# Second down projection token-major, two value groups projected together, attention queries by residue within each half

## The chip, the cores and the metric

The kernel runs on one core of a Trainium2 chip. The metric is device time in microseconds for one execution of the whole program, weights and activations coming from HBM. The engines are TensorE (PE, with its weight loads listed as PEld), VectorE (DVE), ScalarE (ACT), GpSimd (POOL) and SyncE (SP), whose queue issues most of the DMAs.

## The reference, cut to what matters

A two-layer decoder trunk on 256 tokens of 1024 channels, float32. Layer one is a Mamba-2 mixer and a gated FFN with a causal convolution; then keys and values are projected once; layer two is dilated attention and the same kind of FFN; a final RMSNorm gives the output.

```python
ATT_PATTERNS = ((128, 1), (512, 4), (2048, 16))     # window, dilation: three groups
# 8 heads and 2 key/value heads in each group, head size 128
...
for layer in range(DEPTH):
    ...
    x = x + _dilated_mixer(_rms_norm(x, b_norm[j]), k_sh, v_sh, att_w_q[j], att_w_o[j], positions)
    x = x + _conv_ffn(_rms_norm(x, ffn_norm[layer]), ffn_w_up[layer], ffn_conv_w[layer], ffn_w_down[layer])
return _rms_norm(x, final_norm)
```

In group 0 a query sees the last 129 tokens. In group 1 it sees earlier tokens with its own index modulo 4, in group 2 those with its own index modulo 16. One softmax runs over all three groups. The FFN has 2816 hidden channels (22 tiles of 128).

## The kernel before, in words

The residual stream `X` is held channel-major: 128 partitions x 8 channel tiles x 256 tokens. Every projection is exact to float32 by splitting both operands into a high and a low part (fp32r): each product is three matmuls, high x high, high x low, low x high. Weights come in 1 MB pieces (`raw`) by the SP queue and are split on chip by `split` (L93 to L98): ACT rounds the high part (L95), DVE subtracts for the low part (L97). Three `raw` buffers and six `wh`/`wl` pairs of 1024 columns rotate.

TensorE's order is written by hand in the program. The other engines' instructions are ordered by a list scheduler that takes what is ready, earliest in the program first.

**Down projection** (`res_proj`, L606): for both FFNs a stationary 128x128 weight tile meets all 256 tokens. The high weight takes the high and the low operand side by side, one matmul of 512 columns (L625), and the low weight takes the high operand, one of 256 columns (L627). `finish` (L642) adds the result to `X` and, in the second FFN, scales with the final norm's weight into `XW` (L652, L657) and squares. After the last tile `turn` transposes `XW` to token-major (16 transposes, L927), the sums of squares are reduced by small matmuls (L934), POOL takes the power (L942), ACT and DVE scale (L950, L947), and SP stores four blocks of 256 KB (L951).

**Values**: `v_mm(p)` projects one group's 256 value columns for both halves of the tokens, with 256-column matmuls (L262 to L264). Group 1 comes first, the last two channel tiles of both halves last (`late_last`), then the norm's statistics (`nm.stats`, L214), then groups 2 and 0. Groups 1 and 2 go to DRAM and are read back as `Vs`, by residue class modulo 4.

**Attention**: queries stand by residue modulo 4 over all 256 tokens (four classes of 64), so each half of 128 queries holds two classes. For each head `q_tile` projects three groups (24 matmuls of 256 columns each, L242 to L244), and `scores` (L849) computes, for each half, one matmul against all 256 keys of group 0 (L854) and four of 64 queries x 64 keys for groups 1 and 2 (L859), adds a mask and takes the maximum (L863), the exponential (L868) and the normalisation (L870). `p_transpose` (L873) makes three 128x128 transposes for each half (L878); `values` (L883) sums over group 0 with two matmuls of 256 columns (L888) and over groups 1 and 2 with four of 64 (L892), and ACT and DVE split the result into `OT` (L895, L896). Attention operands are plain float32; each of their matmuls is listed as two. TensorE's order around head h is:

```python
q_tile(h, hs[h], 0)
if h > 1:
    p_transpose(h - 2, hs[h - 2])
q_tile(h, hs[h], 1)
if h:
    scores(h - 1, hs[h - 1])
q_tile(h, hs[h], 2)
if h > 1:
    values(h - 2, hs[h - 2])
```

The last two heads' steps are hooks inside the output projection `w_o`, whose `finish` puts its result back into token order.

Of the kernel before, what the change touches and what calls it, by code (L numbers as in the profile page):

```python
# [12 lines left out]
T = 256  # L13
# [15 lines left out]
for _g in range(NG):  # L29
# [3 lines left out]
        ("final_norm", 8), ("ssm_norm", 16), ("dt_bias", 32), ("a_log", 32), ("dskip", 32),  # L33
# [3 lines left out]
_ATT = [("mask", 768), ("cos", 256), ("sin", 256), ("cosp", 256), ("sinp", 256)]  # L37
# [15 lines left out]
def trunk(ctx, tc, a, out):  # L53
# [46 lines left out]
    class Weights:  # L100


        def __init__(self):
# [5 lines left out]
            self.seq += [(("w_v", p), a["w_v"][p], 1024) for p in (1, 2, 0)]  # L109
# [8 lines left out]
        def ffn(self, L):  # L118
            self.seq += [((f"w_up{L}", j), a[f"w_up{L}"][j], 1024) for j in range(FT)]
            self.res(f"w_down{L}", FT)  # L120
# [54 lines left out]

    class Stream:


        def __init__(self, ws):
            self.ws = ws  # L180
            self.h = []
            self.l = []
            for i in range(len(ws)):
# [4 lines left out]
        def add(self, k):  # L188
            for i, w in enumerate(self.ws):
                h, l, x = self.h[i][:, k, :], self.l[i][:, k, :], X[:, k, :]  # L190
                if w == "b_norm":
                    h, l, x = by_class(h), by_class(l), x.rearrange("p (i r) -> p i r", r=4)
                hi_lo(h, l, x, P(w)[:, k:k + 1])
# [60 lines left out]
    def tile_b(po, units, xh, xl, n, c, ks=range(KT), clear=True, **kw):  # L254

        t = slice(c * 128, c * 128 + 128)
        kper = KT // len(units)
# [348 lines left out]
    def res_proj(w, nk, operand, late, S, facc=None, perm=False, first=2, hooks={}):  # L606
# [35 lines left out]
        def finish(n, ys):  # L642
            x = X[:, n, :]
            if perm:
                x = x.rearrange("p (i r) -> p i r", r=4)
            for y in ys:
                DVE.tensor_tensor(out=x, in0=by_class(y) if perm else y, in1=x, op=ALU.add)  # L647
            x = X[:, n, :]
            if S is not None:
                S.add(n)  # L650
            elif n < KT - 1:
                ACT.activation(out=XW[:, n, :], in_=x, func=AF.Copy, scale=P("final_norm")[:, n:n + 1])  # L652
                add_sq(facc, n)
            else:
                lastsq.append(wk.tile([128, T], F32, tag="sq", name="sq"))
                ACT.activation(out=lastsq[0], in_=x, func=AF.Square)
                DVE.tensor_scalar(out=XW[:, n, :], in0=x, scalar1=P("final_norm")[:, n:n + 1],  # L657
                                  scalar2=None, op0=ALU.mult)
# [27 lines left out]
    lastsq = []  # L686
    XW = None

    def ffn(L, S, nxt, facc=None):
        nonlocal XW  # L690
# [28 lines left out]
        for j in range(FT):  # L719
# [11 lines left out]
            if j == 1:  # L731
                ops.append(normed(f"ffn_norm{L}", nm.row))
        if nxt is None:
            XW = act.tile([128, KT, T], F32, tag="xh0", name="XW")
        res_proj(f"w_down{L}", FT, lambda k: g[k // 2][:, k % 2 * 2:k % 2 * 2 + 2, :],
                 [20, 21], nxt, facc)
# [6 lines left out]

    accp = act.tile([128, T], F32, tag="sqp", name="accp")
    DVE.tensor_copy(out=by_class(accp), in_=SA.acc.rearrange("p (i r) -> p i r", r=4))
# [3 lines left out]
    mask = act.tile([128, 2, 384], F32, tag="dec8", name="mask")  # L749
    SP.dma_start(out=mask.rearrange("p c s -> p (c s)"), in_=a["att"][:, :768])  # L750
    trig = act.tile([32, 1024], F32, tag="dec9", name="trig")
    SP.dma_start(out=trig, in_=a["att"][0:32, 768:])

    def C(n):
        return trig[:, ATT[n][0] - 768:ATT[n][1] - 768]

# [12 lines left out]
    def k_post(p, po):  # L769
        kt = KTt[p]  # L770
        sx = "p" if p else ""
        for i in range(2):
            d, x, y = kt[:, i, :], po[:, i, :], nm.row
            if p:
                d = by_class(d)
                x, y = (v.rearrange("p (i r) -> p i r", r=4) for v in (x, y))
            DVE.tensor_tensor(out=d, in0=x, in1=y, op=ALU.mult)
        sh = wk.tile([32, 2, T], F32, tag="cvxs", name="shk")
        DVE.stream_shuffle(out=sh, in_=kt[0:32], mask=rot)
        sn, cs = (C(n + sx).unsqueeze(1).to_broadcast([32, 2, T]) for n in ("sin", "cos"))  # L780
# [4 lines left out]
    def v_mm(p):  # L785
        us, po = W.get("w_v", p), acc_bank()
        if p == 1:
            late_last(lambda c, **kw: tile_b(po[:, c, :], us, xh, xl, 256, c, **kw))
            return po
# [4 lines left out]
    def v_post(p, po):  # L794
        vt = V0
        if p:
            vt = wk.tile([128, 2, T], F32, tag="cvbc", name="vt")
        for c in range(2):
            ACT.activation(out=vt[:, c, :], in_=po[:, c, :], func=AF.Copy, scale=nm.col[:, c:c + 1])
            if p:  # L800
                SP.dma_start(out=vd[128 * c:128 * c + 128, 256 * (p - 1):256 * p], in_=vt[:, c, :])
        if p:
            SP.dma_start(out=Vs[64 * (p - 1):64 * p],
                         in_=vd.rearrange("(i r) f -> i r f", r=4)[:, :, 256 * (p - 1):256 * p])

    po = v_mm(1)
    nm.stats()
    v_post(1, po)
    po = v_mm(2)
    nm.bcast()  # L810
    v_post(2, po)
    v_post(0, v_mm(0))
# [35 lines left out]

    def scores(h, st):  # L849
# [217 lines left out]
```

## Time and profile before

| what | value |
|---|---|
| time, median of 3 runs | 794.57 us (794.43 to 795.48) |
| the profiled execution's own time | 796.08 us |
| its span, first to last instruction | 794.3 us |
| busy: PE, PEld | 774.3 us (97%), 742.7 us (94%) |
| busy: DVE, ACT, POOL | 619.5 us (78%), 478.6 us (60%), 160.6 us (20%) |
| chain that ended last, by engine | PE 75%, DVE 11%, POOL 4%, ACT 4%, issue 3%, DMA 2% |

The chain that ended last is followed back from the last instruction. Busy time of PE is that of overlapping instructions; the distance between the starts of two neighbouring matmuls is what one costs in a dense stretch.

### The profile page before, as it was taken

The numbers are of one execution on the slowest core, as the hardware profiler recorded it, in microseconds if no ns is written. First come the engines' busy times: TensorE is split into PE (matmuls) and PEld (weight loads), VectorE is DVE, ScalarE is ACT, GpSimd is POOL, SyncE is SP. The second block draws the span as 40 slices with busy tenths as digits, with TensorE's granted clock in tenths as the row PEclk, the third lists the DMA queues.
The fourth block names the chain that finished last, engine by engine and source line by source line (L and its number), as shares of the span: only waits on it lengthen the run. The fifth ranks groups of instructions, "written<-read, shape, count | busy, mean of one in ns | idle before, by whom it ended". The sixth has DMA issues, their size and how long they took to land.

```text
span 794.3 us, 14954 instructions
## 1 busy us (share of the span) xinstructions
PE 774.3 (97%) x5992; PEld 742.7 (94%) x5992; DVE 619.5 (78%) x1004; ACT 478.6 (60%) x806; POOL 160.6 (20%) x141
## 2 busy tenths in 40 slices
PE   8999799999999999999999999999999999999997
PEld 7898799999989999999889999999999999999886
DVE  5888979788496999887677598878668999887551
ACT  7846568777375776655555446555466766565441
POOL 0323436543324400000011032211124300000010
PEclk9999989999999999999999999999999999999999
DMA  8484543363454366554556644334325465545521
GB/s 296 169 321 165 203 153 106 109 212 113 154 201 171 106 238 213 186 183 163 196 179 225 222 160 156 115 129 159 108 61 205 149 226 209 199 160 177 177 85 53
DMA packets 22886, 135.31 MB, mean 170 GB/s; under 512 B 2529, under 2 KB 4097, under 8 KB 8865
## 3 DMA queue, kind: packets, MB, share of 16 engines
q1 hardware_dynamic: 21616, 130.14, 47.0%
q10 hardware_dynamic: 1200, 4.23, 1.5%
q8 instruction: 47, 0.77, 0.4%
q14 instruction: 23, 0.18, 0.1%
HBM read 132.75 MB, written 1.61 MB: 169 GB/s over the span
## 4 chain that ended last, share of the span: by engine, by line
PE 75%; DVE 11%; POOL 4%; ACT 4%; issue 3%; DMA 2%; SPq 0%; DVEq 0%; ACTq 0%; POOLq 0%
PE po L242 15%; PE po L243 15%; PE po L244 15%; PE po L625 12%; PE po L627 6%; DVE wl L97 6%; PE po L633 4%; DVE cv L286 2%; PE s L854 1%; DVE xl L169 1%; POOL rs L537 1%; PE py L524 1%; PE op L888 1%; ACT wh L95 1%; PE op L892 1%
## 5 line engine op out<-in xcount | busy, mean ns | idle before, releaser
L97 DVE TENSOR_TENSOR wl<-raw,wh 128x1024 fp32r<-128x1024 f32 (+1 forms) x242 | 307.8, 1278 | 64.0 <-ACT wh L95 63.1
L95 ACT CAST wh<-raw 128x1024 fp32r<-128x1024 f32 (+1 forms) x242 | 247.7, 1034 | 170.5 <-PE po L243 87.0
L243 PE MATMUL po<-xnl,wh 128*128 128x256 f32 x800 | 227.0, 284 | 1.1 <-DVE xnl L319 1.1
L242 PE MATMUL po<-xnh,wh 128*128 128x256 f32 x800 | 227.0, 284 | 0.0
L244 PE MATMUL po<-xnh,wl 128*128 128x256 f32 x800 | 227.0, 284 | 0.0
L242 PEld LDWEIGHTS po<-xnh,wh 128*128 128x128 f32 x800 | 152.8, 191 | 0.3 <-issue 0.2
L243 PEld LDWEIGHTS po<-xnl,wh 128*128 128x128 f32 x800 | 151.2, 189 | 1.3 <-DVE xnl L319 1.3
L244 PEld LDWEIGHTS po<-xnh,wl 128*128 128x128 f32 x800 | 151.2, 189 | 0.1
L625 PE MATMUL po<-gp,wh 128*128 128x512 f32 x352 | 123.3, 393 | 0.0
L286 DVE SCALAR_TENSOR_TENSOR cv<-po,prm,cv 128x255 f32<-128x255 f32 (+2 forms) x232 | 105.8, 476 | 14.1 <-ACT cv L282 12.6
L242 PE MATMUL po<-xh,wh 128*128 128x256 f32 x400 | 115.0, 288 | 0.0
L243 PE MATMUL po<-xl,wh 128*128 128x256 f32 x400 | 113.2, 283 | 0.5 <-DVE xl L169 0.5
L244 PE MATMUL po<-xh,wl 128*128 128x256 f32 x400 | 113.0, 283 | 0.0
L627 PE MATMUL po<-gp,wl 128*128 128x256 f32 x352 | 98.5, 280 | 0.0
L625 PEld LDWEIGHTS po<-gp,wh 128*128 128x128 f32 x352 | 66.0, 187 | 15.4
L242 PEld LDWEIGHTS po<-xh,wh 128*128 128x128 f32 x400 | 76.3, 191 | 0.6
L243 PEld LDWEIGHTS po<-xl,wh 128*128 128x128 f32 x400 | 76.0, 190 | 0.7 <-DVE xl L169 0.7
L244 PEld LDWEIGHTS po<-xh,wl 128*128 128x128 f32 x400 | 75.9, 190 | 0.0
L627 PEld LDWEIGHTS po<-gp,wl 128*128 128x128 f32 x352 | 66.2, 188 | 0.0
L202 POOL TENSOR_TENSOR sqacc<-sqacc,sq 128x256 f32<-128x256 f32 x21 | 19.9, 946 | 217.0 <-ACT sq L201 216.7
L647 DVE TENSOR_TENSOR X<-po,X 128x256 f32<-128x256 f32 x52 | 20.9, 420 | 24.4 <-PE po L627 17.4
L202 POOL TENSOR_TENSOR facc<-facc,sq 128x256 f32<-128x256 f32 x6 | 4.5, 752 | 157.6 <-ACT sq L201 157.6
(207 smaller groups left out, 1270.4 us busy)
## 6 DMA issues: line engine op xcount, KB each, us to landing
raw<-w_up SPq DMA_DIRECT2D x44, 1024.0 KB, 4.8
raw<-w_down SPq DMA_DIRECT2D x16, 1024.0 KB, 4.8
raw<-w_xs SPq DMA_DIRECT2D x8, 1024.0 KB, 4.8
raw<-w_bc SPq DMA_DIRECT2D x8, 1024.0 KB, 4.8
raw<-w_out SPq DMA_DIRECT2D x8, 1024.0 KB, 4.8
raw<-w_q SPq DMA_DIRECT2D x8, 1024.0 KB, 5.1
raw<-w_z SPq DMA_DIRECT2D x7, 1024.0 KB, 6.2
raw<-w_down SPq DMA_DIRECT2D x8, 768.0 KB, 4.2
```

The costliest lines, as they stand in the source:

```text
L95: ACT.copy(out=wh[:, :n], in_=raw)
L97: DVE.tensor_tensor(out=wl[:, :n], in0=raw, in1=wh[:, :n].bitcast(F32), op=ALU.subtract)
L169: DVE.scalar_tensor_tensor(out=xl, in0=x, scalar=w, in1=xh.bitcast(F32), op0=ALU.mult, op1=ALU.subtract)
L202: POOL.tensor_tensor(out=acc, in0=acc, in1=sq, op=ALU.add)
L242: PE.matmul(po, lhsT=wh, rhs=xh, start=start, stop=False, **kw)
L243: PE.matmul(po, lhsT=wh, rhs=xl, start=False, stop=False, **kw)
L244: PE.matmul(po, lhsT=wl, rhs=xh, start=False, stop=stop, **kw)
L286: r = DVE.scalar_tensor_tensor(out=dst[:, i, s:], in0=u[:, i, :T - s], scalar=w[i][:, taps - 1 - s:taps - s], in1=dst[:, i, s:], op0=ALU.m ...
L625: PE.matmul(p.rearrange("p c t -> p (c t)"), lhsT=wh[:, c], rhs=y.rearrange("p c t -> p (c t)"), start=st, stop=False, skip_group_check=True)
L627: PE.matmul(p[:, 1, :], lhsT=wl[:, c], rhs=y[:, 0, :], start=False, stop=sp, skip_group_check=True)
L633: PE.matmul(p[:, o, :], lhsT=l[:, c], rhs=y[:, x, :], start=st and q == 0 and not o, stop=sp and q == 2, skip_group_check=True)
L647: DVE.tensor_tensor(out=x, in0=by_class(y) if perm else y, in1=x, op=ALU.add)
```

## The change

The second FFN's down projection turns its operands round: 128 tokens of the hidden activation are stationary and 512 output channels move, for each of two channel halves, 22 hidden tiles and two token halves, three matmuls of 512 columns each (264 in all). Its result is token-major, so `X` is transposed instead of `XW`: 16 transposes, four after each of the up projection's tiles 6 to 9. The last block of hidden tiles is finished for tokens 0 to 127 first and then for 128 to 255. The final norm's weight is loaded as a row to all partitions.

The values of groups 1 and 2 are projected together, 512 columns in each matmul, and the statistics come after them.

Attention queries stand by residue modulo 4 within each half of 128 tokens. So the first half needs only the first 128 keys of group 0 and 32 of each class. Keys stay in token order and are read with a step of four elements by the small matmuls, eight of 32 queries for each half. `p_transpose` makes two and three transposes. `values` works on two heads at once, in seven matmuls, and writes its result in token order, with a step of four elements in PSUM; it comes before `scores` at every odd head from 3.

```diff
-            self.seq += [(("w_v", p), a["w_v"][p], 1024) for p in (1, 2, 0)]
+            self.seq += [(("w_v", i), a["w_v"][i], 1024) for i in range(3)]
...
+    def v_mm():
+        po = [acc_bank("vo").rearrange("p c f -> p (c f)") for _ in range(2)]
+        us = []
+        for ks in (range(4), range(4, 6), range(6, 8)):
+            if ks.start < 6:
+                us += W.get("w_v", ks.start // 4)
+            for c in range(2):
+                tile_b(po[c], us, xh, xl, 512, c, ks=ks)
+        return po
...
         for c in range(2):
+            n0, n = 128 + 128 * c, 192 + 192 * c
             s = ps.tile([128, 512], F32, tag=f"t{1 + c}", name="s")
-            PE.matmul(s[:, 0:256], lhsT=q[:, 0, 128 * c:128 * c + 128], rhs=KTt[0][:, kv, :],
+            t = slice(128 * c, 128 * c + 128)
+            PE.matmul(s[:, 0:n0], lhsT=q[:, 0, t], rhs=KTt[0][:, kv, 0:n0],
                       start=True, stop=True)
             for g in (1, 2):
-                for r in (0, 1):
-                    t = slice(128 * c + 64 * r, 128 * c + 64 * r + 64)
-                    PE.matmul(s[64 * r:64 * r + 64, 192 + 64 * g:256 + 64 * g], lhsT=q[:, g, t],
-                              rhs=KTt[g][:, kv, t], start=True, stop=True)
+                o = s[:, n0:n].rearrange("p (c g i) -> p c g i", c=1 + c, g=2)[:, :, g - 1, :]
+                k = KTt[g][:, kv, :].rearrange("p (c i r) -> p c i r", c=2, r=4)
+                for r in range(4):
+                    PE.matmul(o[32 * r:32 * r + 32], lhsT=q[:, g, 128 * c + 32 * r:128 * c + 32 * r + 32], rhs=k[:, 0:1 + c, :, r],
+                              start=True, stop=True)
...
-    def values(h, st):
+    def values(h):
+        op = ps.tile([128, 2, T], F32, tag="t5", name="op")
+        ov = op.rearrange("p h (c i r) -> p h c r i", c=2, r=4)
+        pv = pts.rearrange("p h (x r i) -> p h x r i", x=5, r=4)
+        for e in range(2):
+            PE.matmul(ov[:, e], lhsT=V0[:, 0, vc], rhs=pv[:, e, 0:3:2], start=e == 0, stop=False,
                       skip_group_check=True)
+        PE.matmul(ov[:, :, 1], lhsT=V0[:, 1, vc], rhs=pv[:, :, 3], start=False, stop=False,
+                  skip_group_check=True)
         for r in range(4):
+            PE.matmul(ov[:, :, :, r], lhsT=Vs[:, r, vc], rhs=pv[:, :, 1::3, r], start=False,
+                      stop=r == 3, skip_group_check=True)
...
         if h:
+            if h > 2 and h % 2:
+                values(h - 3)
             scores(h - 1, hs[h - 1])
         q_tile(h, hs[h], 2)
-        if h > 1:
-            values(h - 2, hs[h - 2])
...
+             first=4, hooks={7: lambda: scores(AH - 1, hs[AH - 1]), 4: lambda: p_transpose(AH - 2, hs[AH - 2]),
                              17: lambda: p_transpose(AH - 1, hs[AH - 1]),
-                             22: lambda: values(AH - 1, hs[AH - 1])})
+                             21: lambda: values(AH - 2)})
...
+    def turn(i):
+        c, f = i % 2, i // 2
+        if i == 0:
...
+            SP.dma_start(out=tok["w"][:, 0, :], in_=a["fnorm"].unsqueeze(0).to_broadcast([128, D]))
+        for n in range(4):
+            PE.transpose(pt[:, n * 128:n * 128 + 128], X[:, 4 * f + n, c * 128:c * 128 + 128], ident)
+        ACT.copy(out=tok["x"][:, c, 512 * f:512 * f + 512], in_=pt)
...
+        def part(c, q, y, o):
+            DVE.tensor_tensor(out=o, in0=y, in1=o, op=ALU.add)
+            sq = wk.tile([128, 512], F32, tag="C", name="fsq")
+            ACT.activation(out=sq[:, :o.shape[-1]], in_=o, func=AF.Square, accum_out=sm[:, c, q:q + 1])
+            if q:
+                DVE.scalar_tensor_tensor(out=ms[:, c, q:q + 1], in0=sm[:, c, q:q + 1], scalar=1.0 / D,
+                                         in1=ms[:, c, q - 1:q], op0=ALU.mult, op1=ALU.add)
...
+            for q in range(2):
+                h = slice(256 * q, 256 * q + 256)
+                part(c, 1 + q, po[:, h], o[:, h])
+            y = wk.tile([128, 512], F32, tag="cvbc", name="yw")
+            DVE.tensor_tensor(out=y, in0=o, in1=wf, op=ALU.mult)
+            r = col[:, c:c + 1]
+            POOL.tensor_tensor(out=r, in0=ms[:, c, 2:3], in1=nhalf[:, 0:1], op=ALU.pow)
+            ACT.activation(out=yw[c], in_=yw[c], func=AF.Copy, scale=r)
+            DVE.tensor_scalar(out=y, in0=y, scalar1=r, scalar2=None, op0=ALU.mult)
+            for eng, f, y in ((SP, 1, y), (ACT, 0, yw[c])):
+                eng.dma_start(out=out[128 * c:128 * c + 128, 512 * f:512 * f + 512], in_=y)
...
+            def step(k, c):
+                wh, wl = us[k // 2]
+                o, t = slice(k % 2 * 512, k % 2 * 512 + 512), slice(128 * c, 128 * c + 128)
+                x = operand(k)
+                PE.matmul(po[c], lhsT=x[:, 0, t], rhs=wh[:, o], start=k == 0, stop=False)
+                PE.matmul(po[c], lhsT=x[:, 1, t], rhs=wh[:, o], start=False, stop=False)
+                PE.matmul(po[c], lhsT=x[:, 0, t], rhs=wl[:, o], start=False, stop=k == FT - 1)
```

Smaller edits follow from these: `k_post` works on both heads of a group in one instruction and in token order, the query operand is written in two pieces of 128 tokens for each channel tile, `w_o` needs no reordering in `finish`, and mask and tables change with the order.

## Rows read from the trace of the kernel before

**Rows 1.** Busy time by stretch: PE, PEld, DVE, ACT, POOL, clock, DMA share, GB/s.

```profile
490.00:503.00 13.00, 13.00 (x111) 12.10 (x110) 11.91 (x27) 8.08 (x15) 2.73 (x3) 1.00 0.37 122
...
640.00:660.00 20.00, 20.00 (x169) 20.00 (x168) 19.41 (x35) 13.79 (x24) 0.00 (x0) 1.00 0.65 236
...
730.00:785.00 55.00, 55.00 (x317) 48.11 (x316) 24.55 (x32) 21.54 (x32) 3.77 (x5) 1.00 0.31 106
```

**Rows 2.** TensorE's timeline in one head: start us, us, what.

```profile
493.25 0.59 PE L854 MATMUL s<-KTt,q 128*128 128x256 f32 x2
493.78 0.45 PE L859 MATMUL s<-KTt,q 128*64 128x64 f32 x8
494.16 0.70 PE L854 MATMUL s<-KTt,q 128*128 128x256 f32 x2
...
495.17 0.39 PE L242 MATMUL po<-xh,wh 128*128 128x256 f32 x1
...
498.15 1.03 PE L888 MATMUL op<-pts,V 128*128 128x256 f32 x4
499.01 1.00 PE L892 MATMUL op<-pts,Vs 128*128 128x64 f32 x8
499.82 0.37 PE L242 MATMUL po<-xh,wh 128*128 128x256 f32 x1
```

**Rows 3.** Timeline of the end, all engines.

```profile
784.93 0.39 PE L625 MATMUL po<-gp,wh 128*128 128x512 f32 x1
...
785.16 0.28 PE L627 MATMUL po<-gp,wl 128*128 128x256 f32 x1
...
785.28 0.82 PE L927 MATMUL fin<-cst,XW 128*128 128x128 f32 x6
785.48 0.88 DVE L647 TENSOR_TENSOR X<-po,X 128x256 f32<-128x256 f32 x2 [1.22 <-PE po L627]
...
786.46 0.42 ACT L656 ACTIVATE sq<-X 128x256 f32<-128x256 f32 x1 [1.34 <-DVE X L647]
...
787.81 0.70 POOL L942 TENSOR_TENSOR fcol<-ms,nhalf 128x2 f32<-128x2 f32 x1 [1.81 <-DVE ms L939]
788.54 1.26 ACT L950 ACTIVATE O<-fin,fcol 128x512 f32<-128x512 f32 x2 [1.67 <-POOL fcol L942]
...
789.26 1.92 SPq L951 DMA_DIRECT2D out<-O  x4
```

**Rows 4.** DMA view, 780 to 794.4 us in 40 slices of 0.36 us.

```profile
GB/s 0 0 0 0 0 0 0 0 0 0 0 0 0 0 0 0 0 0 0 0 0 0 0 0 0 0 0 0 358 376 381 376 381 376 404 262 0 0 0 0
```

**Rows 5.** TensorE's timeline where the first value group ends.

```profile
436.82 0.28 PE L264 MATMUL po<-wl,xh 128*128 128x256 f32 x1
437.36 0.61 PE L214 MATMUL ss<-ones,sqacc 128*128 128x1 f32 x4 [0.26 <-POOL sqacc L202]
```

**Rows 6.** Matmuls on `po`, 719 to 727 us: first and last start.

```profile
L625 PE MATMUL po<-gp,wh x10: 392/393/394, 723.7 to 726.8; 128*128 128x512 f32 x10
```

**Rows 7.** The chain that ended last, heads 0 and 1.

```profile
482.93 0.63 PE s L854 x2
489.88 0.66 PE ptr L878 x6
```

**Rows 8.** Groups by line and form: busy us, mean ns.

```profile
L534 ACT ACTIVATION_READ_ACCUMULATOR xd<-y 128x1 f32 x16 | 3.0, 188 | 0.0
```

**Rows 9.** TensorE's timeline of the eight small matmuls, cut to ever later windows.

```profile
493.94 0.29 PE L859 MATMUL s<-KTt,q 128*64 128x64 f32 x4
...
494.00 0.23 PE L859 MATMUL s<-KTt,q 128*64 128x64 f32 x2
```

**Rows 10.** Two lines' durations: ns minimum/median/maximum.

```profile
L777 DVE TENSOR_TENSOR KTt<-po,rbc x6: 415/607/618, 456.2 to 469.3; 128x256 f32<-128x256 f32 x6
...
L647 DVE TENSOR_TENSOR X<-po,X x52: 410/420/426, 218.9 to 785.9; 128x256 f32<-128x256 f32 x52
```

**Rows 11.** VectorE's timeline: the normalisations of heads 0 and 1 that come last.

```profile
489.08 0.42 DVE L870 TENSOR_SCALAR pm<-pm,dn 128x384 f32<-128x384 f32 x1
...
502.36 0.40 DVE L870 TENSOR_SCALAR pm<-pm,dn 128x384 f32<-128x384 f32 x1
```

More of the change, by code (lines that the diff above doesn't have):

```diff
@@ L643, in finish @@
             x = X[:, n, :]
-            if perm:
-                x = x.rearrange("p (i r) -> p i r", r=4)
             for y in ys:
[L647 to L658, printed above, removed]
+                DVE.tensor_tensor(out=x, in0=y, in1=x, op=ALU.add)
+            S.add(n)
         n0, steps = 0, 0
@@ L847, in q_tile @@
             q_rope(st["q"], st["sh"], po[:, :gs.stop - gs.start, :], gs)
+    P0 = [wk.tile([128, 512], F32, tag="zs", bufs=4, name="p0") for _ in range(2)]
+    for p in P0:
+        POOL.memset(p[:, 192:256], 0.0)
     def scores(h, st):
@@ L873, in p_transpose @@
     def p_transpose(h, st):
-        pts = wk.tile([128, 3, T], F32, tag="B", bufs=3, name="pts")
+        if h % 2 == 0:
+            pair[h // 2] = act.tile([128, 2, 640], F32, tag="xh0", name="pts")
+        pts = pair[h // 2]
         for c in range(2):
             pt = ps.tile([128, 512], F32, tag=f"t{3 + c}", name="ptr")
-            for b in range(3):
+            for b in range(2 + c):
                 PE.transpose(pt[:, b * 128:b * 128 + 128], st["p"][c][:, b * 128:b * 128 + 128], ident)
-            (DVE.tensor_copy if c else ACT.copy)(
-                out=pts[:, :, c * 128:c * 128 + 128], in_=pt[:, :384].rearrange("p (b q) -> p b q", b=3))
@@ L881, in p_transpose @@
-        st["pts"] = pts
-    def values(h, st):
-        kv, pts = h // 4, st["pts"]
-        vc = slice(kv * 128, kv * 128 + 128)
-        op = ps.tile([128, 512], F32, tag="t5", name="op")
-        for b in range(2):
-            PE.matmul(op[:, 0:256], lhsT=V0[:, b, vc], rhs=pts[:, b, :], start=b == 0, stop=False,
+            n = 256 + 128 * c
+            (DVE.tensor_copy if c else ACT.copy)(out=pts[:, h % 2, 256 * c:256 * c + n], in_=pt[:, :n])
+    def values(h):
+        kv, pts = h // 4, pair[h // 2]
+        vc = slice(kv * 128, kv * 128 + 128)
+        op = ps.tile([128, 2, T], F32, tag="t5", name="op")
[3 more added lines that the diff above has]
+            PE.matmul(ov[:, e], lhsT=V0[:, 0, vc], rhs=pv[:, e, 0:3:2], start=e == 0, stop=False,
@@ L889, in values @@
                       skip_group_check=True)
+        PE.matmul(ov[:, :, 1], lhsT=V0[:, 1, vc], rhs=pv[:, :, 3], start=False, stop=False,
+                  skip_group_check=True)
         for r in range(4):
-            t = slice(64 * r, 64 * r + 64)
-            PE.matmul(op[:, t], lhsT=Vs[:, r, vc], rhs=pts[:, 2, t], start=False, stop=r == 3,
-                      skip_group_check=True)
-        oh, ol = (OT[h // 2][:, h % 2, i, :] for i in range(2))
-        ACT.copy(out=oh, in_=op[:, :T])
@@ L896, in values @@
-        DVE.tensor_tensor(out=ol, in0=op[:, :T], in1=oh.bitcast(F32), op=ALU.subtract)
+            PE.matmul(ov[:, :, :, r], lhsT=Vs[:, r, vc], rhs=pv[:, :, 1::3, r], start=False,
+                      stop=r == 3, skip_group_check=True)
+        oh, ol = (OT[h // 2][:, :, i, :] for i in range(2))
+        ACT.copy(out=oh, in_=op)
+        DVE.tensor_tensor(out=ol, in0=op, in1=oh.bitcast(F32), op=ALU.subtract)
     hs = [{} for _ in range(AH)]
@@ L930, in trunk @@
-    turn(range(3))
-    ss = [acc_bank("fss") for _ in range(2)]
-    for i, q in enumerate((facc, lastsq[0])):
-        for c in range(2):
-            PE.matmul(ss[c][:, 0, 0:1], lhsT=q[:, c * 128:c * 128 + 128], rhs=ones[:, 0:1],
-                      start=i == 0, stop=i == 1)
-    turn(range(3, KT))
-    ms = wk.tile([128, 2], F32, tag="ms", name="ms")
-    for c in range(2):
-        DVE.tensor_scalar(out=ms[:, c:c + 1], in0=ss[c][:, 0, 0:1], scalar1=1.0 / D, scalar2=EPS,
-                          op0=ALU.mult, op1=ALU.add)
```

202 lines of the change are left out of this document (115 added, 87 removed).

## The prediction, made before the change was run

> **What bounds the kernel now.** I read the busy times by stretch first, then TensorE's timeline inside a stretch, then the timeline of the end. In every stretch that the change touches, TensorE is busy for the whole of it at full clock: in one head of attention, in the second up projection and in the second down projection [rows 1]. VectorE is close behind in attention (11.91 of 13 us in this head). So up to the last matmul a microsecond of TensorE's stream is a microsecond of the kernel, and everything else counts only where it makes TensorE wait.
>
> What one head costs is read from starts [rows 2]. A query tile (24 matmuls of 256 columns) lasts from 495.17 to 498.15, so 0.119 us a matmul with a little for the change of kind. The scores last from 493.25 to 495.17: 0.53 us for the first 256-column product until the small ones begin, 0.38 us for the four small ones, 1.01 us for the second half. The values last from 498.15 to 499.82: 0.86 us for two products of 256 columns (four passes, 0.215 us each) and 0.81 us for four of 64 columns, eight passes of 0.10 us although they have a quarter of the columns. Those small ones pay for something other than columns, and all have 128 columns of weights to load.
>
> The end is a chain over all engines [rows 3]. The last down-projection matmul starts at 785.16 and the span ends at 794.3, 9.1 us later: two adds, a square, small matmuls, the power on POOL, scalings, and four stores. The stores move 1.05 MB between 790.1 and 792.9 at about 376 GB/s [rows 4]; 1.3 us more pass until the span ends.
>
> **The change part by part: values projected together.** Before, 96 matmuls of 256 columns at 0.1195 us, 11.47 us. After, 48 of 512. The one 512-column price in sight is a start-to-start of 0.23 us (784.93 to 785.16 [rows 3]), so 11.04 us: **-0.4 us**. Then a stall goes. The statistics' matmuls should start at 436.94 and start at 437.36, since POOL's sum of squares is not done [rows 5]. In the new order 5.5 us of matmuls more stand ahead of them, so **-0.4 us**. The last two channel tiles, which are normalised last, also come 7.7 us after the start instead of 3.8 us, so no new wait there. The first value bank must be evicted before the key projection takes it again: cover falls from about 10 us to 5.1 us (group 0), and a norm, a power and two copies need about 4 us. I cost that at nothing; without the cover it would be at most 1 us.
>
> **Down projection.** Before, it starts at 723.7 [rows 6] and its last matmul ends its slot at 785.28: 61.5 us for 176 pairs. After, 264 matmuls of 512 columns at 0.23 us, 60.7 us: **-0.8 us**. The bounds: 0 if the price is 0.233, and -1.9 us if the extra of a 512-column matmul over its columns is only that of a 256-column one (0.2258 us). Weights are taken at the same rate (1 MB per 5.5 us), the SP queue issues the same number of pieces plus one load of the norm row; ACT and DVE are less than half busy there [rows 1].
>
> The 16 transposes move from the end, where they ran in the shadow of the adds and the power, into the up projection, where TensorE has no gap [rows 1]. Six transposes take 0.66 us [rows 7], so 16 take 1.76 us, with four changes of kind **+1.8 us** (up to +2.3). Their copies (four of 512 columns on ACT, 0.6 us each) hide: ACT has 6 us in 20 free there.
>
> At the seam of the two channel halves the second half's second bank is the first half's first one; DVE must have added it within 1.4 us, and may be inside a weight split of 1.2 us: **+0.2 us** (0 to +0.6).
>
> **The end.** Counting from the last matmul's start: the output is seen 0.43 us later (512 columns). Two adds of 256 columns, 0.44 us each [rows 3]; the squares on ACT follow one behind, 0.42 us each, with 0.19 us for reading the sum [rows 8]; the scalar step about 0.2 us. That puts the mean square at 2.3 us. The product with the norm row fits on DVE beside the squares. Power 0.70 us, scaling 0.63 us [rows 3]: both last stores are issued at about 3.7 us, one on SP, one on ACT. The bytes start 0.85 us behind the issue (789.26 to 790.1), 0.52 MB at 376 GB/s take 1.4 us, and 1.3 us close the span: 7.25 us in place of 9.14, **-1.9 us**. The first 128 tokens' chain and stores are hidden behind 18 matmuls (4.1 us) of the other 128; without that cover the last stores queue and the gain falls to -1.0. Bounds -2.5 and -1.0.
>
> **Attention.** *Transposes*: five in place of six, -0.11 us a head, **-0.9 us** for eight. *Dense scores*: in the first half 128 keys in place of 256, two passes of 0.107 us less, **-1.7 us**. *Small scores*: eight products in place of four in each half. In the old stream the last four matmul entries begin at 493.94 and the last two at 494.00 [rows 9], so two passes (two halves of the array side by side) per 0.055 us; eight passes take 0.22 us, the rest of the 0.38 us is the change of kind and stays. The trace has no product of 32 query columns. Low bound: four quarters of the array run side by side, or the shorter loads and columns shorten the slot, so 16 passes cost 0.22 us and nothing is added. High bound: one pass per slot, 0.88 us in each half, +10.6 us in all. I take the same two passes per 0.055 us, 0.44 us in each half, which is the nearest row's rate: **+3.5 us**.
>
> *Values*: for two heads the new products have 3 x 256 + 4 x 128 = 1280 columns, twice 5 passes of 256 columns at 0.215 us: 2.15 us, and the 14 weight loads at 0.10 us hide under it. Before, two heads took 3.34 us. Four pairs: **-4.8 us**, if writing PSUM with a step of four elements costs nothing. No matmul in the trace writes or reads with a step. The nearest rows are VectorE's [rows 10]: writing keys to SBUF in class order takes 0.607 us, in order 0.415 us; but `finish`, which reads PSUM both in order and with a step, shows 410 to 426 ns for all 52. So low bound no cost; high bound, twice the time, +3.7 instead of -4.8. I take no cost: a pass here gets a column through only every 0.84 ns, half the rate of the fp32r products, so a step has slack to hide in.
>
> *Waits*: between the end of a head's scores and its transposes there were 7.6 us, with values inside; now 5.9 us, two query tiles. The old trace shows that window once: the second half's dense scores of head 0 begin at 482.93, so its scores end 1.01 us later, at 483.94, and with no values behind them its transposes come at 489.88 [rows 7], 5.9 us on; its last normalisation ends at 489.50 [rows 11], in time. Head 1, with the long window, ends its own at 502.76, just before it is needed: DVE's order follows the need. DVE also has less to do (192 columns for 384 in the first half). At the end of attention, `scores` of head 7 comes 0.4 us sooner behind the last query tile, and `values` of the last pair comes three steps (1.1 us) ahead of its user, with 512 columns to copy and subtract, 1.3 us. Together **+0.6 us** (0 to +2).
>
> **Sum**: -0.4 -0.4 -0.8 +1.8 +0.2 -1.9 -0.9 -1.7 +3.5 -4.8 +0.6 = -4.8 us. From the profiled execution's own 796.08 us that gives 791.3 us; the median of the runs is 1.5 us lower, so I forecast 789.8 us.
>
> **Rivals.** (a) *Steps in PSUM cost*: each pass of `values` takes twice as long, 4.3 us a pair, 1 us more than two heads took before. Then the sum is -4.8 + 8.6 = +3.8 us, about 798.4 us, slower. It decides from a pass of 0.335 us on: the 4.8 us over 40 passes are 0.12 us each. For it: the strided key write on DVE [rows 10]; against it: the strided PSUM reads there, and the half rate of these passes. The Trainium skill states it as a rule: PSUM — Partial Sum Buffer, section Specifications (TRN2), has lines of 8 bytes and says that "any non-contiguous AP slows matmuls significantly"; no run here shows it, and VectorE's reads don't agree. (b) *Small products of 32 queries run one pass per slot*, 0.88 us a half: +7.0 us on my sum, about 796.8 us, slower. For it: twice the instructions, and keys read with a step; against it: half as many weight columns to load. (c) *The softmax is late*: if the second half's normalisation came as late as in head 1, 7.6 us after the scores, less 0.5 us of shorter work, TensorE would wait 1.2 us at four to six heads: +5 to +7 us, about 795, no change or slower. Against it: head 0. (d) *The gain at the end is not there* since the last store's closing dominates, and small products cost 0.2 us a head more than forecast: about 793.5 us, no change.
>
> **How the numbers follow.** A measurement here can tell about 0.2%, 1.6 us, from no change. Forecast 0.60; (a) 0.18; (b) 0.07; (c) 0.08; (d) 0.07. Faster: the forecast and a small part of (d), 0.62; no change: the rest of (d), half of (c) and weak forms of (a), 0.14; slower 0.24. The forecast's own range, with four-fold overlap of the small products (-3.5) or worse waits (+2), is 785.5 to 792.5; to hold 8 in 10 it reaches up into (a) and (b), to 798.
>
> **What would show it.** The first matmul entries of the last `values` group and of the query tile behind it, 2.15 us apart for a pair: if 4 us, (a). The scores of a head from first to last, about 2.15 us: if over 2.8 us, (b). TensorE idle ahead of the transposes, with DVE's normalisation as releaser: (c). From the last matmul's start to the span's end 7.2 us. The second down projection's starts 0.23 us apart. The prediction is wrong if stepped accesses or the 32-column products are dearer than their nearest rows, or if the waits move to a place that I costed at nothing.

## The result

The changed kernel took 790.2 us (median of 4 runs, 789.49 to 792.25) beside 794.85 us (794.43 to 795.48) for the kernel before: ratio 0.9945, 95% interval 0.9925 to 0.9965. The forecast was 789.8 us. A second set of 5 runs gave 790.59 beside 795.28 us, ratio 0.9937 (0.9924 to 0.9949). So the change makes the kernel faster by about 0.6%.

The profiled execution after took 792.25 us with a span of 790.5 us, 3.8 us less than before. The work ahead of the change must be taken out first. The first value matmul starts at 431.14 us before, at 432.23 after, and at 430.69 in a second profile of the very same changed kernel: up to that point two executions of one program differ by 1.5 us. From there on the stages can be laid side by side: in that second profile the first two of them last 50.85 and 115.82 us, in the first 50.84 and 115.81. All entries but the span's end are starts in TensorE's timeline of the two executions.

| from ... to ... | before | after | difference | forecast |
|---|---|---|---|---|
| first value matmul to first score matmul | 431.14 to 481.95 | 432.23 to 483.07 | +0.03 | -0.8 |
| to the last statistics' matmuls ahead of the second FFN | to 601.75 | to 598.88 | -3.99 | -3.3 |
| to the first matmul of the second down projection | to 723.69 | to 722.56 | +1.74 | +1.8 |
| to its last matmul | to 785.16 | to 783.50 | -0.53 | -0.6 |
| to the end of the span | to 794.3 | to 790.5 | -2.14 | -1.9 |
| sum | 363.16 us | 358.27 us | -4.89 | -4.8 |

The sum agrees to 0.1 us, but the first two rows show that it does so with errors of opposite sign in it: 0.8 us too hopeful in the first, 0.7 us too cautious in the second. Now the views of the profile after, in the order of the stages.

All waits of TensorE from 425 us to the end (us in all, times, longest). The third row, at the start of the second up projection, was there before, too; the other three are new:

```profile
PE ptr L906 <- DVE pm L892: 1.4, 4, 0.4
PE ss L230 <- ACT rbc L250: 0.9, 1, 0.9
PE po L259 <- DVE xl L175: 0.5, 1, 0.5
PE po L649 <- DVE OT L927: 0.2, 1, 0.2
```

The largest single one stands where the keys' projection begins. Timeline after, all engines (start, us, what, idle time before it and what ended it):

```profile
449.35 0.60 PE L247 MATMUL pb<-dg,ones 128*128 128x256 f32 x2
449.49 1.05 ACT L95 CAST wh<-raw 128x1024 fp32r<-128x1024 f32 x1 [0.40 <-PE po L279]
450.44 0.36 ACT L250 COPY rbc<-pb 128x256 f32<-128x256 f32 x1
...
450.86 0.61 PE L230 MATMUL ss<-ones,accp 128*128 128x1 f32 x4 [0.91 <-ACT rbc L250]
...
451.32 0.36 PE L258 MATMUL po<-xh,wh 128*128 128x256 f32 x1
```

`nmp.stats()` makes a second set of statistics, that of the keys' norm, into the PSUM bank in which `pb` stands, the broadcast of the first norm. ACT's copy `rbc` must empty the bank, and ACT began a 1.05 us weight cast 0.14 us after the broadcast started. Before, the broadcast came one value group earlier, at 443.65, and the second statistics at 449.83. So the stall of [rows 5] went, and a longer one came a step later, from another cause.

One pair of `values` and one `scores`, which answer to [rows 2]; TensorE's timeline after:

```profile
506.44 1.03 PE L918 MATMUL op<-pts,V 128*128 128x256 f32 x4
507.30 0.59 PE L920 MATMUL op<-pts,V 128*128 128x256 f32 x2
507.73 1.05 PE L923 MATMUL op<-pts,Vs 128*128 128x128 f32 x8
508.62 0.39 PE L873 MATMUL s<-KTt,q 128*128 128x128 f32 x2
508.94 0.43 PE L880 MATMUL s<-KTt,q 128*32 128x32 f32 x16
509.29 0.70 PE L873 MATMUL s<-KTt,q 128*128 128x256 f32 x2
509.92 0.65 PE L880 MATMUL s<-KTt,q 128*32 128x64 f32 x16
510.50 0.39 PE L258 MATMUL po<-xh,wh 128*128 128x256 f32 x1
```

Values for two heads last from 506.44 to 508.62, 2.18 us (forecast 2.15; 3.34 before). The scores last 1.88 us (1.92 before, forecast 2.15): 0.32 and 0.63 us of dense products, and 0.35 and 0.58 us until the next kind of work for the two sets of small ones.

The price of 512 columns in the second down projection, 264 matmuls (ns minimum/median/maximum, first and last start):

```profile
L1010 PE MATMUL fo<-wh,gp x88: 389/394/402, 722.6 to 783.0; 128*128 128x512 f32 x88
...
L1012 PE MATMUL fo<-wl,gp x88: 387/394/400, 723.0 to 783.5; 128*128 128x512 f32 x88
```

From 722.56 to 783.50 are 263 steps, 0.2317 us each. All of them are 0.22 to 0.24 us, so the seam of the two channel halves, for which the prediction added 0.2 us, costs nothing. Last, the end, which answers to [rows 3]:

```profile
783.50 0.39 PE L1012 MATMUL fo<-wl,gp 128*128 128x512 f32 x1
783.93 0.76 DVE L973 TENSOR_TENSOR xt<-fo,xt 128x256 f32<-128x256 f32 x2 [1.23 <-PE fo L1012]
784.39 0.42 ACT L975 ACTIVATE fsq<-xt 128x256 f32<-128x256 f32 x1 [1.46 <-DVE xt L973]
...
785.83 0.55 POOL L996 TENSOR_TENSOR fcol<-ms,nhalf 128x1 f32<-128x1 f32 x1 [3.65 <-DVE ms L977]
786.41 0.72 ACT L997 ACTIVATE wf<-wf,fcol 128x512 f32<-128x512 f32 x1 [1.12 <-POOL fcol L996]
...
787.17 0.34 ACTq L1000 DMA_DIRECT2D out<-wf  x1
```

and the DMA view from 776 to 790.6 us, 40 slices of 0.365 us, which answers to [rows 4]:

```profile
GB/s 0 0 0 45 0 0 0 0 0 0 0 0 0 0 0 0 0 0 0 0 73 404 399 415 146 0 0 0 0 0 0 0 275 393 427 337 6 0 0 0
```

The first 128 tokens' bytes move from 783.3 to 785.1, so they are out of the way. The last two stores are issued at 786.93 on SP (by its timeline from 785.6 us on) and at 787.17 on ACT, the second 3.67 us behind the last matmul's start (forecast 3.7). Their bytes move from about 787.8 to 789.1, and the span ends 1.4 us later, about as before.

### The profile page after: what moved, and what is told of

Its sections match the earlier page's. It is cut to its first block, busy times and chain, and to the rows that moved or that the text cites. A ratio compares the mean times of both kernels' runs of the same rounds, so it can differ in the third digit from the quotient of the medians.

```text
span 790.5 us, 14796 instructions
## 1 busy us (share of the span) xinstructions
PE 767.6 (97%) x5928; PEld 729.9 (92%) x5928; DVE 612.5 (77%) x1001; ACT 475.1 (60%) x807; POOL 158.2 (20%) x138
## 4 chain that ended last, share of the span: by engine, by line
PE 72%; DVE 11%; ACT 6%; POOL 4%; issue 4%; DMA 2%; SPq 0%; POOLq 0%; ACTq 0%; DVEq 0%
PE po L258 14%; PE po L260 14%; PE po L259 14%; PE po L641 7%; DVE wl L97 5%; PE po L649 4%; PE po L643 4%; PE fo L1010 2%; PE fo L1012 2%; PE fo L1011 2%; DVE cv L302 2%; ACT wh L95 1%; PE s L880 1%; POOL rs L553 1%; PE s L873 1%
## 5 line engine op out<-in xcount | busy, mean ns | idle before, releaser
L641 PE MATMUL po<-gp,wh 128*128 128x512 f32 x176 | 61.6, 393 | 0.0
L643 PE MATMUL po<-gp,wl 128*128 128x256 f32 x176 | 49.3, 280 | 0.0
L641 PEld LDWEIGHTS po<-gp,wh 128*128 128x128 f32 x176 | 33.0, 187 | 7.7
L1010 PE MATMUL fo<-wh,gp 128*128 128x512 f32 x88 | 34.7, 394 | 0.0
L1011 PE MATMUL fo<-wh,gp 128*128 128x512 f32 x88 | 34.7, 394 | 0.0
L1012 PE MATMUL fo<-wl,gp 128*128 128x512 f32 x88 | 34.6, 394 | 0.0
```

What stands on the lines that cost most here:

```text
L641: PE.matmul(p.rearrange("p c t -> p (c t)"), lhsT=wh[:, c], rhs=y.rearrange("p c t -> p (c t)"), start=st, stop=False, skip_group_check=True)
L643: PE.matmul(p[:, 1, :], lhsT=wl[:, c], rhs=y[:, 0, :], start=False, stop=sp, skip_group_check=True)
L1010: PE.matmul(po[c], lhsT=x[:, 0, t], rhs=wh[:, o], start=k == 0, stop=False)
L1011: PE.matmul(po[c], lhsT=x[:, 1, t], rhs=wh[:, o], start=False, stop=False)
L1012: PE.matmul(po[c], lhsT=x[:, 0, t], rhs=wl[:, o], start=False, stop=k == FT - 1)
```

## The experiments

The theory at the start was the prediction's own sum, corrected by the trace: the small products and the values at the sizes above, the new wait at the statistics 0.9 us, the transposes' waits 1.4 us. The rivals were that the parts lean on each other, that stepped PSUM accesses do cost something that another gain hides, and that the scores are set by something other than their columns.

**The down projection alone.** The kernel before with `turn`, `out_proj` and the row-wise final norm; values and attention as before.

> The kernel before with the second down projection turned token-major alone (its transposes of X in the up projection, its new end). Theory (the stages add up, as the two traces' landmarks say): transposes +1.8 us, the projection's own matmuls -0.45, the end -2.25, together -0.9 us, ratio 0.999. Rival (the gain of the whole change lies at the end, and attention gives its own back): -2 us or more, ratio 0.9975 or less. TensorE's starts 0.2275 to 0.235 us apart in the down projection, the span ends 6.8 us after the last matmul's slot by the theory.

Measured: 794.81 beside 795.12 us, ratio 0.9998 (0.9989 to 1.0007). In its trace the time from the first value matmul (430.40) to the end (792.9) is 362.5 us, 0.7 us less than before. The end alone gains 1.9 us (785.62 to 792.9) and the matmuls 0.5; the transposes take 1.7 back. The time can't tell 0.7 us from nothing, but its interval leaves no room for the rival's 2 us.

**Values alone.**

```diff
-            self.seq += [(("w_v", p), a["w_v"][p], 1024) for p in (1, 2, 0)]
+            self.seq += [(("w_v", i), a["w_v"][i], 1024) for i in range(3)]
...
+                tile_b(po[c], us, xh, xl, 512, c, ks=ks)
```

> The kernel before with only the values of groups 1 and 2 projected together. Theory: the wider matmuls save 0.55 us and the statistics' wait of 0.42 us goes, but the second statistics now follow the broadcast directly in the same PSUM bank and wait 0.9 us for its copy behind a weight split: 0.0 us, ratio 1.000. Rival (my prediction's sum, no new wait): -0.85 us, ratio 0.9989, and no idle TensorE ahead of the second statistics.

Measured: 795.2 us, ratio 0.9999 (0.999 to 1.0008). From the first value matmul to the first score matmul 50.85 us, as in the changed kernel. So the rival's -0.85 us is not there, and the wait is this edit's own:

```profile
PE ss L218 <- ACT rbc L238: 0.9, 1, 0.9
```

**Attention alone.** Queries by residue within halves, `scores`, `p_transpose`, `values` and `k_post` as changed; the rest as before.

> The kernel before with only the new query order, score and value products of attention. Theory: -4.0 us, ratio 0.995 (values -4.6, dense scores -1.7, transposes -0.9, small products +1.4, waits at the transposes and at the output projection about +2). Rival (the parts help each other: the waits at the transposes come from the shifted weight stream of the joint values): -5.5 us, ratio 0.993, and no TensorE idle ahead of the transposes of heads 0, 1, 3 and 5.

Measured: 791.74 us, ratio 0.9955 (0.9943 to 0.9968), 3.4 us less. From the first score matmul to the last statistics 115.81 us, as in the changed kernel. The transposes' waits are the same 1.4 us at four heads, so they come from attention itself and not from its neighbours. The three parts by their traces (-0.7, 0.0, -4.0) come to -4.7 of the -4.9 us, which leaves next to nothing for an interaction. The times of the runs are blunter: the three medians add up to -3.6 us beside -4.7 for the whole, and their intervals are as wide as that difference.

**A step in PSUM at full rate.** In the changed kernel, the query projections are computed in bfloat16 from the upper halves of the same operands, so the queries are less exact. Group 0 writes PSUM in order, group 1 with a step of four elements, group 2 with a step of two.

```diff
+        d = po[:, g % 2, :].rearrange("p (r i) -> p r i", r=4)
+        if g:
+            n = 4 if g == 1 else 2
+            d = po[:, g % 2, :].rearrange("p (i r) -> p r i", r=n)
```

> The changed kernel with the query projections computed in bf16 from the high halves of the operands' bits, so its queries are other numbers: tile 0 of each head writes PSUM in order, tile 1 with a step of four elements, tile 2 with a step of two; all read alike. Theory (a step costs PSUM twice the time, and the float32 passes of values only hide it at half rate): tile 0 about 0.11 to 0.12 us a matmul, tiles 1 and 2 about 0.21 us, the span some 35 us longer. Rival (a step in PSUM costs nothing at any rate): all three tiles at the same 0.11 to 0.12 us, the span within 1 us.

Measured: 826.5 us (one execution), 36 us more than the changed kernel, as the theory said. TensorE's timeline in group 2 of one head, in group 0 of the next, and in its group 1 behind the transposes:

```profile
528.11 0.42 PE L258 MATMUL po<-xh,wh 128*128 128x256 bf16 x1
...
529.84 0.42 PE L260 MATMUL po<-xh,wl 128*128 128x256 bf16 x1
...
531.01 0.28 PE L260 MATMUL po<-xh,wl 128*128 128x256 bf16 x1
...
532.71 0.28 PE L260 MATMUL po<-xh,wl 128*128 128x256 bf16 x1
...
534.19 0.42 PE L259 MATMUL po<-xl,wh 128*128 128x256 bf16 x1
...
536.35 0.42 PE L260 MATMUL po<-xh,wl 128*128 128x256 bf16 x1
```

The pairs of lines are 8, 15 and 10 matmuls apart. In order a matmul of 256 columns takes 0.113 us, with a step of two (first pair) and of four (last pair) 0.216 us. That is just what one of the two passes of a float32 matmul takes in order (0.215 us). The step halves a rate that float32 does not reach.

**No steps in attention.** In the changed kernel, the small products read the keys in stored order and `values` writes its result without the step, so queries meet other keys and the result stands in another order.

```diff
-                k = KTt[g][:, kv, :].rearrange("p (c i r) -> p c i r", c=2, r=4)
+                k = KTt[g][:, kv, :].rearrange("p (c r i) -> p c i r", c=2, r=4)
...
-        ov = op.rearrange("p h (c i r) -> p h c r i", c=2, r=4)
+        ov = op.rearrange("p h (c r i) -> p h c r i", c=2, r=4)
```

> The changed kernel with the value products writing PSUM in order and the small score products reading keys in order, so its attention mixes other tokens. Theory (float32 passes have the slack for a step): a pair's values 2.15 to 2.2 us and the small score products of the second half 0.58 us as in the changed kernel, the time within 1 us of it. Rival (the step costs something where the columns are few): the second half's 16 passes fall from 0.58 towards 0.40 us, the span about 1.5 us shorter; values shorter than 2.1 us would speak for a cost in PSUM.

Measured: 788.05 us (one execution). One pair and one `scores`:

```profile
504.09 1.03 PE L918 MATMUL op<-pts,V 128*128 128x256 f32 x4
...
506.27 0.39 PE L873 MATMUL s<-KTt,q 128*128 128x128 f32 x2
506.59 0.33 PE L880 MATMUL s<-KTt,q 128*32 128x32 f32 x16
506.85 0.70 PE L873 MATMUL s<-KTt,q 128*128 128x256 f32 x2
507.48 0.43 PE L880 MATMUL s<-KTt,q 128*32 128x64 f32 x16
507.84 0.39 PE L258 MATMUL po<-xh,wh 128*128 128x256 f32 x1
```

The values take 2.18 us (504.09 to 506.27) with the PSUM step or without: it costs nothing. The scores fall from 1.88 to 1.57 us, all of it in the small products (0.35 to 0.26, 0.58 to 0.36). So the step that costs is the one with which the keys are *read*, 0.31 us a head: the theory holds for the write, the rival for the read.

**A stepped read at full rate.** In the changed kernel the query projections read their moving operand with a step of four elements in SBUF (so the queries' tokens are in another order).

```diff
+            v = [t[:, k, :].rearrange("p (i r) -> p r i", r=4) for t in (xh, xl)]
+            mm3(d, wh[:, c], wl[:, c], v[0], v[1], start=k == 0, stop=k == KT - 1)
```

> The changed kernel with the query projections (fp32r) reading their moving operand with a step of four elements in SBUF and writing PSUM in order, so its queries stand in another order. Theory (reads are like writes: at full rate a step doubles a matmul): 0.21 us a matmul for all 576 of them, the span some 50 to 55 us longer. Rival (only PSUM minds a step): 0.12 us a matmul, the span within 1 us.

Measured: 853.02 us (one execution). TensorE's timeline:

```profile
505.29 0.42 PE L260 MATMUL po<-xh,wl 128*128 128x256 f32 x1
...
507.62 0.40 PE L911 MATMUL ptr<-cst,p 128*128 128x128 f32 x2
```

Ten matmuls in 2.33 us, 0.233 us each in place of 0.1195. That is dearer than the theory's 0.21, and the run is 63 us longer than the changed kernel instead of 50 to 55. The Trainium skill, SBUF — State Buffer, section Specifications (TRN2), has lines of 16 bytes and wants two hits on each for full bandwidth; a step of four float32 elements hits each once, and the trace agrees. A smaller step was not tried, so no run here shows where the price begins.

**Statistics later.** In the changed kernel:

```diff
-    nmp.stats()
     for p in range(3):
-        k_post(p, k_mm(p))
+        po = k_mm(p)
+        if p == 0:
+            nmp.stats()
+        k_post(p, po)
```

> The changed kernel with the second statistics moved behind the first key projection. Theory (the statistics wait 0.9 us in the broadcast's PSUM bank): TensorE's idle ahead of them goes, about -0.9 us against the changed kernel, ratio to the kernel before about 0.9935. Rival (the key projection then waits as long for the broadcast or for a bank): no change against the changed kernel, ratio 0.9945, the idle time elsewhere.

Measured: 789.15 us beside 795.04, ratio 0.9924 (0.9904 to 0.9944). The wait on `rbc` is gone, and from the first value matmul to the first score matmul it is 49.67 us in place of 50.84: 1.2 us, 0.3 more than the wait as listed. The list counts idle time from the end of the last matmul, and in a dense stretch the next one starts before that end (0.12 us apart, 0.28 us long), so a stall costs more than its entry.

**Softmax first.** In the changed kernel the softmax of `scores` goes ahead of other work that is ready on DVE and ACT.

```diff
+            with tc.high_priority():
+                DVE.tensor_tensor_reduce(out=pv, in0=s[:, :n], in1=mask[:, 192 * c:192 * c + n], scale=1.0,
...
+                DVE.tensor_scalar(out=pv, in0=pv, scalar1=dn, scalar2=None, op0=ALU.mult)
```

> The changed kernel with the softmax instructions of VectorE and ScalarE put ahead of everything else that is ready. Theory (at the even heads weight splits and rotary work stand ahead of the softmax, and the transposes of heads 0, 1, 3 and 5 wait about 0.4 us each): those waits go, -1.5 us, ratio to the kernel before about 0.9925. Rival (both engines are simply short of time there): the wait moves to the weights or to the queries' rotary part, change within 0.5 us, and TensorE's idle time is named by a weight split or by q.

Measured: 788.92 us, ratio 0.9921 (0.9901 to 0.9941). What made the transposes wait in the changed kernel is seen in its timelines of ACT, DVE and TensorE; the last two lines are the same transposes without a wait, one head on:

```profile
499.62 1.05 ACT L95 CAST wh<-raw 128x1024 fp32r<-128x1024 f32 x1 [1.90 <-PE po L259]
500.70 0.36 ACT L840 COPY q<-po 32x256 f32<-32x256 f32 x1
501.09 0.71 ACT L890 ACTIVATE pm<-pm,nb,sc 128x384 f32<-128x384 f32 x1
...
502.32 0.43 DVE L842 STREAM_SHUFFLE shq<-po 32x256 f32<-32x256 f32 x1
502.66 0.40 DVE L892 TENSOR_SCALAR pm<-pm,dn 128x384 f32<-128x384 f32 x1
...
502.42 0.38 PE L906 MATMUL ptr<-cst,p 128*128 128x128 f32 x2
503.20 0.52 PE L906 MATMUL ptr<-cst,pm 128*128 128x128 f32 x3 [0.40 <-DVE pm L892]
503.48 0.36 PE L258 MATMUL po<-xh,wh 128*128 128x256 f32 x1
...
516.37 0.38 PE L906 MATMUL ptr<-cst,p 128*128 128x128 f32 x2
...
516.84 0.37 PE L258 MATMUL po<-xh,wh 128*128 128x256 f32 x1
```

The exponential stood behind a weight cast and a copy, the normalisation behind a shuffle of the next query; two of the other three stalls show the same order, and at the first head it is a cast, a weight split and the shuffle. From its start to the next query matmul such a set of transposes takes 1.06 us (502.42 to 503.48), without the stall 0.47: 0.59 us lost where the list says 0.40. All four stalls cost 2.2 us (0.43 us at the first head). With the priority they are gone, and attention takes 114.25 us in place of 115.81. What comes in their place is smaller:

```profile
PE s L880 <- DVE q L845: 0.5, 1, 0.5
```

**Keys in class order.** In the changed kernel `k_post` writes the keys of groups 1 and 2 in class order within each half, and `scores` reads them in order:

```diff
+                           ((kt[:, i, :], "p (c r i) -> p c i r"), (po[:, i, :], "p (c i r) -> p c i r"),
...
-                k = KTt[g][:, kv, :].rearrange("p (c i r) -> p c i r", c=2, r=4)
+                k = KTt[g][:, kv, :].rearrange("p (c r i) -> p c i r", c=2, r=4)
```

> The changed kernel with one edit: the keys of groups 1 and 2 are stored in class order within each half, so that the small score products read them in order and the step is taken once by VectorE when it writes the keys. Theory (the moving operand's step of four elements in SBUF costs about 0.09 us in each first half's 16 small passes and 0.22 us in each second half's, 2.5 us for eight heads): 2.0 to 2.7 us less than the changed kernel, ratio to before about 0.9915, and the stretch from a head's first dense score product to the next query tile falls from 1.9 to 1.6 us. Rival 1 (that stretch is set by the change of kind and by the loads of 32 query columns, and the 2.5 us of the kernel without steps came from the other side effects of dropping the order): less than 0.5 us. Rival 2 (shorter scores are given back as waits, since the transposes come 0.3 us sooner behind the softmax and VectorE's stepped writes of the keys, six of about 0.6 us in place of 0.4, delay the first head): the score stretch falls as in the theory, the waits of the transposes rise from 1.4 to over 3 us, and the time falls by less than 1 us.

The changed kernel beside it:

> The changed kernel unaltered, for comparison with the two beside it on one chip: ratio to before 0.9945 (0.9925 to 0.9965), about 790.5 us. In its trace one wait of 0.9 us of the second statistics for ScalarE's copy of the broadcast, and 1.4 us of waits of the transposes for VectorE's scaling.

Measured: 788.22 us, ratio 0.9912 (0.9898 to 0.9925), beside 790.59 us, ratio 0.9937 (0.9924 to 0.9949): 2.4 us less. The scores of one head, 506.84 to 508.40, take 1.56 us:

```profile
506.84 0.39 PE L881 MATMUL s<-KTt,q 128*128 128x128 f32 x2
...
508.40 0.39 PE L258 MATMUL po<-xh,wh 128*128 128x256 f32 x1
```

The transposes' waits are listed at 1.5 us, 0.1 more, so next to nothing is given back, and both rivals fall. Attention takes 113.34 us in place of 115.8.

**All four.** The last three edits together (statistics later, softmax first, keys in class order), and the last head's scores and the last pair's values one step nearer to their user in `w_o`:

```diff
-             first=4, hooks={7: lambda: scores(AH - 1, hs[AH - 1]), 4: lambda: p_transpose(AH - 2, hs[AH - 2]),
+             first=4, hooks={8: lambda: scores(AH - 1, hs[AH - 1]), 4: lambda: p_transpose(AH - 2, hs[AH - 2]),
...
-                             21: lambda: values(AH - 2)})
+                             20: lambda: values(AH - 2)})
```

> The changed kernel with four edits: statistics of the keys' norm behind the first key group's products, the softmax ahead of VectorE's and ScalarE's other work, keys of groups 1 and 2 in class order, and the last scores and values each one step nearer to their user (scores of the last head at step 8, values of the last pair at step 20 of the output projection). If the pieces add: -1.3 us (first), -1.6 us (second), -2.5 us (third) by their single runs and the theory above, -0.3 us for the fourth (the two waits of 0.5 and 0.2 us, less what comes in their place): about 5 us less than the changed kernel, ratio to before about 0.988. Rival (the pieces lean on each other: shorter scores leave the softmax less time, so part of the third is given back): 3 to 4 us less, ratio about 0.990.

Measured: 784.92 us, ratio 0.9866 (0.9851 to 0.9881), 5.7 us less than the changed kernel beside it. All waits of TensorE from 425 us on:

```profile
PE po L259 <- DVE xl L175: 0.5, 1, 0.5
PE s L890 <- DVE q L855: 0.2, 1, 0.2
```

The pieces add: 1.2 us by the statistics (49.66 us to the first scores), 4.7 us in attention (481.92 to 592.98, 111.06 us). The fourth edit was not run on its own: 4.7 less the 1.6 and 2.5 us of the other two leave 0.7 us for it.

## Why the prediction was right, and where it was not

**The total** was right, but that it came out within 0.1 us is luck. Most steps hold: values -4.6 us (four pairs at 2.18 in place of 3.34; forecast -4.8), dense scores -1.7 (0.53 to 0.32 us in the first half; -1.7), transposes of p -0.9 without their stalls (0.47 us for five, 516.37 to 516.84, in place of 0.58 for six, below; -0.9), the 16 transposes +1.74 (+1.8), the down projection -0.53 (-0.6 with the seam), the end -2.14 (-1.9). On the end the chain to the last store's issue came out to 0.03 us; the bytes began 0.85 us behind the first of the two issues, as forecast, which is 0.6 us behind the second. Three terms do not hold, and the sum is right because one of them was too dear by 2.1 us and the other two too cheap by 0.8 and 1.9; small gains and losses make up the rest.

```profile
489.72 0.82 PE L878 MATMUL ptr<-cst,pm 128*128 128x128 f32 x6
490.30 0.36 PE L242 MATMUL po<-xh,wh 128*128 128x256 f32 x1
```

**Small scores** were mis-sized: +3.5 us forecast, +1.4 measured (0.35 + 0.58 us in place of 0.38 twice, eight heads). The step that failed was the rate of two passes per 0.055 us, taken over from products of 64 queries. Without the stepped read, 16 passes take 0.26 and 0.36 us, less than eight took before: that is the low bound of the prediction or better, as four quarters of the array side by side would give. Whether it comes from that or from the shorter loads, no run tells. The step in the keys hid this gain, 2.4 us. That the second half's 0.58 us looks like the forecast's 0.60 (0.38 and 0.22 more) is luck: two effects meet there that the forecast had not told apart, and "keys read with a step", which it named under rival (b), was a real cost, a smaller one.

**Waits** were too low: +0.6 us forecast, 0 to 2 its range, 2.5 measured: 2.2 at the transposes, start to start (1.4 by the list), and 0.3 in the output projection (23.78 us of its matmuls in attention's stretch in place of 23.51), where the last values are late by 0.2. The step that failed is "DVE's order follows the need": it does not, the exponential stood behind a cast and the normalisation behind a shuffle, too late at four heads. This is rival (c) at less than half its price: 2.2 us in place of 5 to 7. What is left of attention's 4.0 us is small: one stall of 0.2 us in the old last head's small products is gone, and the query projections take 62.4 us in place of 62.75, perhaps for fewer changes of kind, which was not tried.

**Values projected together** failed as a term: -0.8 us forecast, 0.0 measured. The matmuls became cheaper and the old stall went, but the second statistics, which the prediction did not cost, wait 0.9 us. The value bank, whose eviction it did look at, had its cover; what was late is the small bank of the broadcast, whose next user came from one value group away to next in line. Moving the statistics behind the first keys gave 1.2 us back.

**Rival (a)** is refuted for this kernel: the pair takes 2.18 us with and without the step in PSUM. The Trainium skill's sentence (PSUM — Partial Sum Buffer, section Specifications (TRN2)) holds at full rate, 0.113 to 0.216 us; it does not hold in float32's passes of 0.215 us, where the step costs nothing. The prediction's reason, that the half rate leaves slack, fits both runs. Rival (b) would have had 0.88 us in each half and the change of kind on top; 0.35 and 0.58 with it were measured. Rival (d) had neither its missing end nor its dearer products.

What stays open: a stepped write at full rate was tried in bfloat16 only, not in the kernel's own fp32r; a stepped read in float32 only in the small products; and why executions of one program differ by 1.5 us ahead of the first value matmul. In the slower of the two profiles the first layer's matmuls wait 0.9 us for POOL once (`py`, L540), in the other they do not; what makes POOL late there was not tried.

## What to carry to other kernels

Price a stepped access by the rate that the pass really reaches: where a pass already runs at half rate a step in its PSUM output was free here, while a step of four float32 elements in the moving operand cost in the small float32 products too, so put the step where another engine writes the operand once. When stages move closer together, list every bank and buffer that the next step reuses, the small ones of statistics and broadcasts too, and ask which engine must empty it and what that engine starts first. Take what a stall costs from start to start, since a list of idle times showed only 1.4 of 2.2 us here. Lay two traces side by side from the first changed instruction, not from the start of the span, or a microsecond of the untouched part is taken for an effect.

## What the runs showed of the hardware

A step of two and a step of four in a bfloat16 matmul's PSUM output cost the same, 0.216 us for 256 columns in place of 0.113. A step of four in the moving operand of an fp32r matmul costs 0.233 us for 256 columns in place of 0.1195. Sixteen float32 passes with 32 query columns and 64 keys each, read in order, take 0.36 us until the next kind of matmul starts; eight passes with 64 query columns and 64 keys took 0.38 us [rows 2].
